# Reordering the eight mLSTM projections, and the squares of the second row tile, in a Trainium2 transformer kernel

## Chip, core and metric

The kernel runs on one core of one Trainium2 chip. The metric is the device time of one execution in microseconds (us), lower is better. The five engines of the core are named as the profile names them: PE (TensorE; PEld is its loading of weights), DVE (VectorE), ACT (ScalarE), POOL (GpSimd) and SP (SyncE, which here only issues DMAs).

## What is computed

Two transformer blocks one behind the other, over 512 positions of 1024 features in float32. The change lies in the first part of the first block, the hybrid mixer:

```
h = rms_norm(x, norm_mix_g)
dq, dk, dv, mq, mk, mv, mo, mi, mf = split(h @ w_in)
y_da = diff_attention(dq, dk, dv)                      # 4 heads
qk   = silu(causal_depthwise_conv([mq, mk]))           # 4 taps, 1024 channels
y_ml = mlstm_chunkwise(qk[:512], qk[512:], mv, mo, mi, mf)   # 4 heads
x    = x + concat(y_da, y_ml) @ w_out
```

In the mLSTM each head multiplies queries with keys, weights the products by gates, multiplies with the values, normalizes, and scales the result by `sigmoid(mo)`. After the mixer come cross-attention over 256 memory rows, a mixture of 32 experts, a norm, and the second block.

## The kernel before

Every float32 product is made of float16 halves: an operand is split into a high half (ACT, line 138) and the remainder (DVE, line 139), and each product is three matmuls (`mm3`, line 110). A weight piece of 1024 x 256 is loaded by SP into a `raw` buffer (line 144) and split in two parts of 128 x 1024 (`load_w`, `wh` and `wl`).

The work stands in program order in `mixer` (line 348): the norm of four row tiles of 128 positions, the projections of the differential attention's values (`values`, line 406) and of its queries and keys (`turned`, line 391), the four heads of the differential attention (`diff_head`, line 520), and `mlstm` (line 583). Then `mem_kv` (line 719) makes keys and values of the memory rows, and `out_proj` (line 477) the output projection.

The order on each engine is not this program order. The framework's scheduler places instructions one after another; of those that its own model takes to be ready, it takes the one that comes first in the program, save where `high_priority` or `after` (line 92: not before these instructions) say otherwise. So while a head of the differential attention waits for DVE or ACT, PE is given matmuls of what comes later in the program: the mLSTM's projections. Each engine is given one list, in the order that comes out of this.

`mlstm` first makes the gates (64 columns), then three kinds of projections, two or four weight pieces each:

- Queries and keys (line 621, four pieces, two blocks of 128 channels each, 24 matmuls of 512 columns a block). A block is followed on ACT by a copy `u` (line 628), a first tap (630), a tanh (635) and a high half, and on DVE by three taps `acc` (line 632), one product `th` (636) and one remainder `mql` (139).
- Values (line 644, two pieces, four row tiles each, 24 matmuls of 256 columns a tile). A tile is followed by one high half on ACT and one remainder `mvl` on DVE.
- Output gates (line 650, two pieces, four row tiles each, 24 matmuls of 256 columns a tile). A tile is followed by one tanh on ACT (`tho`, line 654) and nothing on DVE.

Head h of the mLSTM needs query block h and key block 4 + h, all values, and at its end the output gates. It goes from scores (PE, `tr`), to `W` (DVE, line 678), its halves `ch` and `cl`, and products with the values (PE, `at<-mvh`), to `hr` (DVE, line 699). The PE transposes `tr<-ident,pe` (line 560) and `tr<-ident,yd` (line 474) belong to the differential heads and wait for the DVE rows `pe` (line 553) and `yd` (line 580).

The norm of a row tile (`norm_steps`, line 216) takes two squares with their sums on ACT (line 200), a power on POOL, two scaled halves `xn` on DVE (line 223), eight transposes on PE (line 255), and their halves `xh` (ACT) and `xl` (DVE). Line 357 says which earlier halves a tile's steps wait for.

Of the kernel before, what the change touches and what calls it, by code (L numbers as in the profile page):

```python
# [11 lines left out]
F32 = mybir.dt.float32  # L12
# [8 lines left out]
P = 128  # L21
D = 1024
S = 512
NT = S // P
# [16 lines left out]
W0 = 0, 1  # L41
X0 = 1
LO = 3
EARLY = 0,1,1,1,1,1
WARM = 18
TICKS = [(k, i) for k in range(2) for i in range(NT)], range(14), ((0, 0), (0, 1), (0, 2), (0, 3))
LATE = 2
# [12 lines left out]
def brow(ap):  # L60

    return bass.AP(tensor=ap.tensor, offset=ap.offset, ap=[[0, P], [1, ap.shape[-1]]])


class Kern:
# [192 lines left out]
    def consts(self, low):  # L258
# [23 lines left out]
        pd = self.bank("at")  # L282
        for _ in range(WARM):
            nc.tensor.matmul(pd.rearrange("p (k t) -> p k t", k=4), self.identh,
# [63 lines left out]
    def mixer(self, low, big, pool, early, adp):  # L348
        nc, a = self.nc, self.a
        g = self.g_mix  # L350
        xh = big.tile([P, DC, S], F16, name="xh", tag="A", bufs=2)
        xl = big.tile([P, DC, S], F16, name="xl", tag="A", bufs=2)
        los = []
        ws = []
        with self.tc.high_priority():
            for i in range(NT):
                with self.after(*(self.last_w if i == W0[0] + 2 else ()), *(los[i - 2] if i > 1 else ())):
                    steps = self.norm_steps(low, self.x[i], g, xh, xl, i)
                    next(steps)
                    if i == 0:  # L360

                        ws.append(self.load_w(None, 1024, raw=self.first_w[:, :1024]))
                    for _ in steps:
                        pass
                los.append(self.last)
                if i == W0[0] + 1:
                    with self.after(*los[W0[0]]):
                        ws[0] += self.load_w(None, 1024, raw=self.first_w[:, 1024:])
                if i == W0[1] + 1:
                    with self.after(*los[W0[1]]):  # L370
                        ws.append(self.load_w(a["w_pre"][5]))
        lo = los[LO]
        with self.after(*lo):
            self.mixer_consts(pool)
            self.late_consts()
        ropec = pool.tile([P, S], F32, name="ropec")
        ropes = pool.tile([P, S], F32, name="ropes")
        gateb = pool.tile([64, 1], F32, name="gateb")
        with self.after(*lo):
            nc.scalar.dma_start(ropec, a["rope_cos"])  # L380
            nc.scalar.dma_start(ropes, a["rope_sin"])
            nc.scalar.dma_start(gateb, a["gate_b"])

        mqk = [big.tile([P, 8, S], F16, name=n, tag="C", bufs=2) for n in ("mqh", "mql")]

        qkh = big.tile([P, 8, S], F16, name="qkh", tag="B", bufs=2)
        qkl = big.tile([P, 8, S], F16, name="qkl", tag="B", bufs=2)
        vh = low.tile([P, NT, 512], F16, name="vh", tag="V", bufs=2)
        vl = low.tile([P, NT, 512], F16, name="vl", tag="V", bufs=2)

        def turned(k):
            w = self.load_w(a["w_pre"][k])
            for b in range(2):
                pq = self.proj_feat(w, (xh, xl), 256, b)
                qf = self.t2(pool, "qf", "q")
                nc.scalar.activation(qf, pq, AF.Copy, scale=INV)
                p2 = self.bank("at")
                self.mm(p2, self.swap, qf, True, True)
                t1 = self.t2(pool, "t1", "q")
                nc.gpsimd.tensor_tensor(t1, qf, ropec, OP.mult)  # L400
                t2 = self.t2(pool, "t2", "q")
                nc.vector.tensor_tensor(t2, p2, ropes, OP.mult)
                nc.vector.tensor_tensor(t2, t2, t1, OP.add)
                self.split(t2, qkh[:, 2 * k + b], qkl[:, 2 * k + b], SA)

        def values(k):
            w = ws[k]
            for i in range(NT):
                pv = self.proj_tok(w, (xh, xl), i)
                o = slice(k * 256, k * 256 + 256)  # L410
                self.last = self.split(pv[:, :256], vh[:, i, o], vl[:, i, o], SA * INV)

        self.bank_of_ada = early, "raw"
        self.ada_prio = ADA0
        self.beside = self.ada(adp)

        def ticks():
            for _ in range(next(early_ticks, 0)):
                self.tick()

        early_ticks = iter(EARLY)
        for k in range(2):
            values(k)
            if k == 0:
                self.silu_c(pool)
            ticks()
        for k in range(2):
            turned(k)
            ticks()
            turned(2 + k)  # L430
            ticks()
        lamb = self.t2(pool, "lamb", "q")[:, :256].rearrange("p (a b) -> p a b", a=4)
        nc.scalar.dma_start(lamb.rearrange("p a b -> p (a b)"), brow(a["da_lambda"]))
        lam = self.lam_of(pool, lamb)
        yy = [early.tile([P, DC, S], F16, name=n, tag="raw") for n in ("yyh", "yyl")]
        for h in range(4):
            self.diff_head(low, pool, qkh, qkl, vh, vl, lam, yy, h)
        self.mlstm(pool, xh, xl, *mqk, gateb, yy)
        return yy
# [143 lines left out]
    def mlstm(self, pool, xh, xl, qh, ql, gateb, yy):  # L583
# [33 lines left out]
        nc.scalar.activation(cols[:, 1].rearrange("p k h -> p (k h)"), pc[:, 16:32], AF.Exp)  # L617
        nc.vector.tensor_scalar(cols[:, 1], cols[:, 1], SA, None, op0=OP.mult)


        for k in range(4):
            w = self.load_w(a["w_pre"][6 + k])
            for bb in range(2):
                blk = 2 * k + bb
                pq = self.proj_feat(w, (xh, xl), 256, bb)
                u = pool.tile([P, 3 + S], F32, name="u", tag="u", bufs=2)
                nc.vector.memset(u[:, 0:3], 0.0)
                nc.scalar.activation(u[:, 3:], pq, AF.Copy, scale=INV)
                acc = self.t2(pool, "acc", "q")
                nc.scalar.activation(acc, u[:, 3:], AF.Identity, scale=convw[:, blk, 3:4], bias=convb[:, blk:blk + 1])  # L630
                for j in range(3):
                    nc.vector.scalar_tensor_tensor(acc, u[:, j:j + S], convw[:, blk, j:j + 1], acc,
                                                   op0=OP.mult, op1=OP.add)
                th = self.t2(pool, "th", "q")
                nc.scalar.activation(th, acc, AF.Tanh, scale=0.5)
                nc.vector.scalar_tensor_tensor(th, th, 1.0, acc, op0=OP.add, op1=OP.mult)
                s = 0.5 * SA * (1.0 if blk < 4 else P ** -0.5)
                self.split(th, qh[:, blk], ql[:, blk], s)
# [2 lines left out]
        vl = pool.tile([P, NT, 4, 129], F16, name="mvl")  # L641
        nc.vector.memset(vh[:, :, :, 128:129], 1.0)
        nc.vector.memset(vl[:, :, :, 128:129], 0.0)
        for k in range(2):
            w = self.load_w(a["w_pre"][10 + k])
            for i in range(NT):
                pv = self.proj_tok(w, (xh, xl), i)[:, :256].rearrange("p (h e) -> p h e", h=2)
                self.split(pv, vh[:, i, 2 * k:2 * k + 2, :P], vl[:, i, 2 * k:2 * k + 2, :P], SA * INV)
        tho = pool.tile([P, NT, 512], F32, name="tho")
        for k in range(2):  # L650
            w = self.load_w(a["w_pre"][12 + k])
            for i in range(NT):
                pv = self.proj_tok(w, (xh, xl), i)
                nc.scalar.activation(tho[:, i, k * 256:k * 256 + 256], pv[:, :256], AF.Tanh, scale=0.5 * INV)

        offs = [0, 512, 896, 1152]
        pending = None
        for h in range(4):
# [27 lines left out]
            for g in range(2):  # L686
                pn = self.bank("at")
                pnv = pn[:, :258].rearrange("p (i e) -> p i e", i=2)
                for ii in range(2):
                    i = 2 * g + ii  # L690
# [1298 lines left out]
```

## Time and profile before

| what | value |
|---|---|
| three runs | 1574.32, 1573.76, 1569.97 us |
| median of the runs | 1573.76 us |
| the profiled execution | 1572.59 us |
| its span in the trace | 1570.9 us |
| PE, DVE, ACT busy | 94%, 61%, 38% of the span |
| granted clock of PE, mean | 0.987 |

The profiled execution is 1.17 us below the median. Its span covers the instructions; 1.69 us of its time lie around it. Shares of busy time are means over very different stages, and a stage has to be read by its own window. A busy PE includes time at half clock, which the column PEclk shows (1.00 is 2.4 GHz, 0.50 would be 1.2 GHz).

### The profile page before, as it was taken

How to read it: one execution, taken by the hardware profiler on the slowest of the kernel's cores; microseconds unless marked ns; L12 is line 12 of the kernel's file. 1: busy time of each engine (PE TensorE's matmuls, PEld its weight loads, DVE VectorE, ACT ScalarE, POOL GpSimd, SP SyncE). 2: the span in 40 equal slices, each digit the busy share in tenths (PEclk: the TensorE clock that was granted, in tenths of full speed). 3: DMA queues.
4: the chain of work that ended last, by engine and by line, in shares of the span. 5: the costliest groups of instructions: out<-in, count | busy, mean ns of one | idle time of the engine just before them, and what ended most of it. 6: DMA issues, size and time to landing. Idle time of an engine off the chain costs nothing.

```text
span 1570.9 us, 25373 instructions
## 1 busy us (share of the span) xinstructions
PE 1472.3 (94%) x10268; PEld 815.0 (52%) x10268; DVE 960.3 (61%) x2025; ACT 603.6 (38%) x1256; POOL 102.1 (6%) x120
## 2 busy tenths in 40 slices
PE   8999998899898999999999997898899989989998
PEld 6434676785585444444444443533445774335457
DVE  5769847788855324324324327799475667976562
ACT  5357745423542101101101105642377545226661
POOL 0210001000000000000000002301000012100000
PEclk9999999999999999999999999999999999999999
DMA  8422121788463999999999993232201222340201
GB/s 283 166 81 81 55 81 68 248 339 337 145 265 149 421 421 421 421 421 420 421 421 421 421 420 136 88 111 82 83 28 55 95 75 81 111 128 14 78 28 55
DMA packets 53705, 320.96 MB, mean 204 GB/s; under 512 B 6672, under 2 KB 9552, under 8 KB 17744
## 3 DMA queue, kind: packets, MB, share of 16 engines
q1 hardware_dynamic: 47728, 309.92, 51.0%
q10 hardware_dynamic: 5856, 9.37, 2.1%
q8 instruction: 82, 1.34, 0.3%
q14 instruction: 39, 0.32, 0.1%
HBM read 308.27 MB, written 3.69 MB: 199 GB/s over the span
## 4 chain that ended last, share of the span: by engine, by line
PE 48%; DVE 11%; ACT 4%; issue 3%; DMA 1%; POOL 1%; DVEq 0%; POOLq 0%; ACTq 0%; SPq 0%
PE h L100 13%; PE mm L100 8%; PE y L100 7%; PE cv L100 6%; PE tr L100 3%; PE ga L100 3%; PE at L100 3%; PE po L100 3%; DVE sc L1659 2%; DVE wl L139 2%; DVE m L1658 1%; PE tr L1700 1%; DMA raw<-in_w_big 1%; PE tr L104 1%; DVE sc L1654 1%
## 5 line engine op out<-in xcount | busy, mean ns | idle before, releaser
L100 PE MATMUL h<-raw,xg 128*64 128x512 f32 x1024 | 222.5, 592 | 0.9 <-DVE xg L970 0.9
L100 PEld LDWEIGHTS <-wh 128*128 128x128 f16 x1104 | 107.2, 100 | 134.7 <-issue 41.4
L139 DVE SCALAR_TENSOR_TENSOR wl<-raw,wh 128x1024 f16<-128x1024 f32 (+1 forms) x107 | 134.4, 1263 | 55.5 <-ACT wh L138 55.3
L100 PEld LDWEIGHTS h<-raw,xg 128*64 128x64 f32 x1024 | 73.4, 137 | 146.7 <-issue 141.6
L138 ACT ACTIVATE wh<-raw 128x1024 f16<-128x1024 f32 (+1 forms) x107 | 109.8, 1040 | 75.2 <-PE cv L100 29.7
L1001 DVE SCALAR_TENSOR_TENSOR hm<-hm,h 128x512 f32<-128x512 f32 x16 | 11.0, 687 | 180.5 <-ACT hm L1000 180.5
L100 PE MATMUL y<-raw,hT 128*64 128x512 f32 x512 | 113.6, 595 | 0.0
L1030 DVE SCALAR_TENSOR_TENSOR x<-tr,x 128x512 f32<-128x512 f32 x128 | 86.3, 688 | 11.9 <-PE tr L100 9.9
L100 PEld LDWEIGHTS <-wl 128*128 128x128 f16 x552 | 55.1, 100 | 60.2 <-issue 9.4
L1000 ACT ACTIVATE hm<-h 128x512 f32<-128x512 f32 x16 | 9.6, 597 | 198.5 <-PE h L100 182.8
L100 PE MATMUL cv<-hh,wh 128*128 128x512 f16 x192 | 75.3, 392 | 9.9 <-DVE ga L1388 9.7
L100 PEld LDWEIGHTS <-hh 128*128 128x128 f16 x768 | 72.7, 98 | 15.3 <-ACT hh L138 2.2
L139 DVE SCALAR_TENSOR_TENSOR yl<-y,cw,yh 128x512 f16<-128x512 f32 x32 | 24.0, 751 | 89.0 <-ACT yh L138 89.0
L100 PE MATMUL cv<-hl,wh 128*128 128x512 f16 x192 | 74.9, 390 | 0.0
L100 PE MATMUL cv<-hh,wl 128*128 128x512 f16 x192 | 74.9, 390 | 0.0
L100 PEld LDWEIGHTS y<-raw,hT 128*64 128x64 f32 x512 | 35.2, 137 | 70.3 <-issue 63.8
L100 PEld LDWEIGHTS <-hl 128*128 128x128 f16 x640 | 62.7, 98 | 14.6 <-issue 2.1
L138 ACT ACTIVATE yh<-y,cw 128x512 f16<-128x512 f32 x32 | 22.0, 687 | 114.2 <-PE y L100 112.9
L100 PE MATMUL ga<-Sel,hl 128*128 128x128 f16 x480 | 65.8, 219 | 0.0
L100 PE MATMUL ga<-Sel,hh 128*128 128x128 f16 x480 | 65.7, 219 | 0.0
L1295 DVE CUSTOM_DVE_ANT_0 raw<-raw,cact 128x1024 f32<-128x1024 f32 x48 | 58.7, 1240 | 8.0 <-DMA raw<-in_w_ada 7.1
L100 PE MATMUL mm<-wh,xh 128*128 128x256 f16 x192 | 53.7, 280 | 2.5 <-ACT xh L138 2.4
(437 smaller groups left out, 3422.6 us busy)
## 6 DMA issues: line engine op xcount, KB each, us to landing
raw<-in_w_moe SPq DMA_DIRECT2D x192, 1024.0 KB, 19.8
raw<-in_w_pre SPq DMA_DIRECT2D x33, 1024.0 KB, 4.9
raw<-in_w_big SPq DMA_DIRECT2D x30, 1024.0 KB, 5.0
raw<-in_w_ada SPq DMA_DIRECT2D x24, 1024.0 KB, 7.0
R<-cu ACTq DMA_DIRECT2D x16, 271.0 KB, 6.6
R<-cu SPq DMA_DIRECT2D x16, 271.0 KB, 7.0
x<-in_x_tm SPq DMA_DIRECT2D x4, 512.0 KB
t5d<-t5v SPq DMA_DIRECT2D x1, 1536.0 KB, 10.9
```

The lines of the kernel that those rows point to most:

```text
L100: self.last_mm = self.pin(self.nc.tensor.matmul(out, lhsT, rhs, start=start, stop=stop, skip_group_check=True))
L104: return self.pin(self.nc.tensor.transpose(out, src, ident))
L138: return (nc.scalar.activation(hi, src, func, scale=scale), nc.vector.scalar_tensor_tensor(lo, src, scale, hi, op0=OP.mult, op1=OP.subtract))
L139: nc.vector.scalar_tensor_tensor(lo, src, scale, hi, op0=OP.mult, op1=OP.subtract))
L1000: nc.scalar.activation(hm[:n], ph[0][:n], AF.Tanh, scale=0.5 / SA)
L1001: nc.vector.scalar_tensor_tensor(hm[:n], hm[:n], 1.0, ph[0][:n], op0=OP.add, op1=OP.mult)
L1030: self.last_add = nc.vector.scalar_tensor_tensor(xo, pc, 1.0 / 1024.0, xo, op0=OP.mult, op1=OP.add)
L1295: nc.vector.tensor_tensor_reduce(w, w, cact, 1.0, 0.0, OP.mult, OP.add, to)
L1654: nc.vector.scalar_tensor_tensor(sc, re[:, :W], s, sc, op0=OP.mult, op1=OP.add)
L1658: nc.vector.max(m8, sc)
L1659: nc.vector.match_replace(sc, m8, sc, -3.0e38)
L1700: nc.tensor.transpose(pt[:, (i - k) * P:(i - k + 1) * P], ps_[i][:, k * P:(k + 1) * P], self.ident)
```

## The change

A table `MLSTM` sets the order of the eight projections by kind (0 values, 1 queries and keys, 2 output gates) and piece: both values; the first piece of queries (heads 0, 1) and of keys (heads 0, 1); both output gates; the second piece of queries (heads 2, 3) and of keys. Before it was four of queries and keys, two of values, two of output gates. The computation is the same. In line 357 the second row tile's steps (i = 1) now wait for the first tile's last halves; before, only tiles 2 and 3 had such a wait, for the tile two before.

```diff
+MLSTM = (0, 0), (0, 1), (1, 0), (1, 2), (2, 0), (2, 1), (1, 1), (1, 3)
...
             for i in range(NT):
-                with self.after(*(self.last_w if i == W0[0] + 2 else ()), *(los[i - 2] if i > 1 else ())):
+                with self.after(*(self.last_w if i == W0[0] + 2 else ()), *(los[max(i - 2, 0)] if i else ())):
                     steps = self.norm_steps(low, self.x[i], g, xh, xl, i)
...
-        for k in range(4):
+        def queries_keys(k):
+
             w = self.load_w(a["w_pre"][6 + k])
             for bb in range(2):
                 blk = 2 * k + bb
...
-        for k in range(2):
+        tho = pool.tile([P, NT, 512], F32, name="tho")
+
+        def values(k):
             w = self.load_w(a["w_pre"][10 + k])
...
-        tho = pool.tile([P, NT, 512], F32, name="tho")
-        for k in range(2):
+
+        def output_gates(k):
             w = self.load_w(a["w_pre"][12 + k])
...
+        for step, k in MLSTM:
+            (values, queries_keys, output_gates)[step](k)
```

What it does to the order on PE, counted there: projection matmuls of 256 and of 512 columns between the last `yd` transposes of one differential head and those of the next, and (in brackets) those of them that stand directly ahead of the `yd` transposes, behind the head's last product with values.

| stretch | before: 256 | before: 512 | after: 256 | after: 512 |
|---|---|---|---|---|
| head 0 | 0 | 70 (24) | 124 (28) | 0 |
| head 1 | 0 | 91 (20) | 68 (0) | 29 (10) |
| head 2 | 81 (28) | 31 | 29 (29) | 67 (5) |
| head 3 | 144 (22) | 0 | 149 (32) | 0 |
| behind head 3, ahead of the mLSTM's heads | 159 | 0 | 14 | 96 |

The first place is ACT at the start of the program (`x_82` to `x_85` are the four row tiles, `junk,ss` the squares). Before:

```order
L200 ACTIVATE junk,ss<-x_82 128x512 x2
L138 ACTIVATE wh<-raw 128x1024
L200 ACTIVATE junk,ss<-x_83 128x512 x2
L138 ACTIVATE xh<-tr 128x4x128 x2
L138 ACTIVATE wh<-raw 128x1024
L200 ACTIVATE junk,ss<-x_84 128x512 x2
```

and after:

```order
L201 ACTIVATE junk,ss<-x_82 128x512 x2
L139 ACTIVATE wh<-raw 128x1024
L139 ACTIVATE xh<-tr 128x4x128 x2
L201 ACTIVATE junk,ss<-x_83 128x512
L139 ACTIVATE wh<-raw 128x1024
L201 ACTIVATE junk,ss<-x_83 128x512
L201 ACTIVATE junk,ss<-x_84 128x512 x2
```

The second tile's squares have gone behind the first tile's halves, and its second square also behind the split of the next weight part.

The second place is DVE around the end of differential head 0 and the start of head 1. Before:

```order
L578 TENSOR_SCALAR rs_r<-rs_r 128x4
L632 SCALAR_TENSOR_TENSOR acc<-u,mlc,acc 128x512
L580 TENSOR_TENSOR yd<-at,rs_r 128x512
L550 RECIPROCAL sm<-sm 128x2
L632 SCALAR_TENSOR_TENSOR acc<-u,mlc,acc 128x512
L551 TENSOR_SCALAR sm<-sm,lam 128x1
L632 SCALAR_TENSOR_TENSOR acc<-u,mlc,acc 128x512
L139 SCALAR_TENSOR_TENSOR yyl<-tr,gs,yyh 128x512
L553 SCALAR_TENSOR_TENSOR pe<-pe,sm 128x128
```

and after:

```order
L579 TENSOR_SCALAR rs_r<-rs_r 128x4
L581 TENSOR_TENSOR yd<-at,rs_r 128x512
L551 RECIPROCAL sm<-sm 128x2
L140 SCALAR_TENSOR_TENSOR mvl<-mm,mvh 128x2x128
L552 TENSOR_SCALAR sm<-sm,lam 128x1
L554 SCALAR_TENSOR_TENSOR pe<-pe,sm 128x128
```

Three taps of a convolution block that stood between the head's rows are gone from here, and one values' remainder has come.

The third place is DVE at the start of the mLSTM's head 0 (`ml` and `xn` belong to the norm of the memory rows). Before:

```order
L678 TENSOR_TENSOR W<-tr,W 128x512
L678 TENSOR_TENSOR W<-tr,W 128x384
L678 TENSOR_TENSOR W<-tr,W 128x256
L139 SCALAR_TENSOR_TENSOR cl<-W,ch 128x512
L139 SCALAR_TENSOR_TENSOR cl<-W,ch 128x384
L139 SCALAR_TENSOR_TENSOR ml<-mm,mh 128x4x128
L139 SCALAR_TENSOR_TENSOR cl<-W,ch 128x256
```

and after:

```order
L685 TENSOR_TENSOR W<-tr,W 128x512
L633 SCALAR_TENSOR_TENSOR acc<-u,mlc,acc 128x512
L140 SCALAR_TENSOR_TENSOR ml<-mm,mh 128x4x128 x2
L140 SCALAR_TENSOR_TENSOR cl<-W,ch 128x512
L633 SCALAR_TENSOR_TENSOR acc<-u,mlc,acc 128x512
L685 TENSOR_TENSOR W<-tr,W 128x384
L685 TENSOR_TENSOR W<-tr,W 128x256
L637 SCALAR_TENSOR_TENSOR th<-th,acc 128x512
L140 SCALAR_TENSOR_TENSOR cl<-W,ch 128x384
L140 SCALAR_TENSOR_TENSOR cl<-W,ch 128x256
L140 SCALAR_TENSOR_TENSOR mql<-th,mqh 128x512
```

The last convolution block's rows now stand among the rows of the mLSTM's first head. On PE, eight transposes of the memory rows now stand ahead of this head's first product with the values; before there were five.

## Rows read from the trace of the kernel before

**Rows 1.** The page's first part: busy time and share of the span by engine.

```profile
PE 1472.3 (94%) x10268; PEld 815.0 (52%) x10268; DVE 960.3 (61%) x2025; ACT 603.6 (38%) x1256; POOL 102.1 (6%) x120
```

**Rows 2.** Busy time by stage: differential heads 0 to 3, output gates, mLSTM's heads.

```profile
core 0: us, PE busy (x) PEld busy (x) DVE busy (x) ACT busy (x) POOL busy (x), PEclk, DMA share, GB/s
...
93.00:126.00 33.00, 29.77 (x176) 13.85 (x173) 25.05 (x60) 22.43 (x48) 1.88 (x2) 0.95 0.15 55
126.00:155.00 29.00, 27.64 (x171) 13.41 (x167) 27.28 (x59) 22.83 (x47) 1.92 (x1) 1.00 0.29 96
155.00:180.00 25.00, 23.47 (x188) 14.95 (x185) 23.10 (x54) 17.77 (x41) 1.43 (x1) 1.00 0.17 59
180.00:206.00 26.00, 23.69 (x217) 18.64 (x216) 19.34 (x44) 17.56 (x41) 2.13 (x3) 1.00 0.23 81
206.00:226.40 20.40, 20.40 (x172) 17.66 (x171) 3.37 (x5) 5.82 (x11) 0.00 (x0) 0.92 0.15 53
226.40:291.00 64.60, 57.61 (x469) 41.75 (x468) 51.74 (x109) 35.77 (x84) 8.20 (x8) 0.95 0.31 105
```

**Rows 3.** What PE waited for from 93 to 207 us, the two longest: total, times, longest.

```profile
PE tr L560 <- DVE pe L553: 4.7, 5, 1.9
PE tr L474 <- DVE yd L580: 2.3, 2, 1.3
```

**Rows 4.** The same from 207 to 345 us, the three longest in total.

```profile
PE mm L100 <- DVE kk L139: 1.9, 1, 1.9
PE mm L255 <- DVE ml L139: 1.9, 1, 1.9
PE tr L100 <- DVE W L678: 1.7, 3, 0.8
```

**Rows 5.** Busy time in three short stretches with a low PEclk.

```profile
100.00:105.80 5.80, 5.58 (x21) 2.25 (x21) 3.65 (x10) 5.63 (x14) 0.00 (x0) 0.71 0.00 0
...
207.00:214.00 7.00, 7.00 (x50) 5.66 (x50) 0.92 (x3) 0.95 (x3) 0.00 (x0) 0.76 0.01 2
...
238.00:246.00 8.00, 6.62 (x40) 5.32 (x41) 7.28 (x14) 4.56 (x12) 1.10 (x2) 0.57 0.56 199
```

**Rows 6.** DVE by line and form, 93 to 207 us: busy, mean ns | idle before.

```profile
L632 DVE SCALAR_TENSOR_TENSOR acc<-u,mlc,acc 128x512 f32<-128x512 f32 x24 | 17.8, 743 | 0.0
L139 DVE SCALAR_TENSOR_TENSOR wl<-raw,wh 128x1024 f16<-128x1024 f32 x13 | 15.8, 1219 | 0.9 <-ACT wh L138 0.9
L636 DVE SCALAR_TENSOR_TENSOR th<-th,acc 128x512 f32<-128x512 f32 x8 | 5.5, 688 | 0.8 <-ACT th L635 0.6
L139 DVE SCALAR_TENSOR_TENSOR mql<-th,mqh 128x512 f16<-128x512 f32 x8 | 5.5, 685 | 0.0
...
L139 DVE SCALAR_TENSOR_TENSOR mvl<-mm,mvh 128x256 f16<-128x256 f32 x8 | 3.4, 423 | 0.2
```

**Rows 7.** ACT's timeline around 217 us: start, duration.

```profile
216.11 0.38 ACT L654 ACTIVATE tho<-mm 128x256 f32<-128x256 f32 x1 [0.25 <-PE mm L100]
...
218.73 0.38 ACT L654 ACTIVATE tho<-mm 128x256 f32<-128x256 f32 x1 [1.29 <-PE mm L100]
```

**Rows 8.** The chain that ended last, near 1070 us: start, duration.

```profile
1070.25 5.18 PE mm L100 x24
```

**Rows 9.** Timeline at the start: ACT, PE and DVE.

```profile
10.83 0.63 ACT L200 ACTIVATE junk<-x 128x512 bf16<-128x512 f32 x1 [0.55 <-DMA x<-in_x_tm]
...
12.21 1.06 ACT L138 ACTIVATE xh<-tr 128x512 f16<-128x512 f32 x2
...
14.03 1.40 DVE L223 SCALAR_TENSOR_TENSOR xn<-x,rs_r,grow 128x512 f32<-128x512 f32 x2
```

**Rows 10.** DVE's timeline in the mLSTM's head 0.

```profile
229.55 1.16 DVE L678 TENSOR_TENSOR W<-tr,W 128x512 f32<-128x512 f32 x2 [0.37 <-PE tr L100]
...
234.63 0.42 DVE L699 SCALAR_TENSOR_TENSOR hr<-at,dn 128x256 f32<-128x256 f32 x1
```

**Rows 11.** The costliest groups of the whole span, the first row.

```profile
L100 PE MATMUL h<-raw,xg 128*64 128x512 f32 x1024 | 222.5, 592 | 0.9 <-DVE xg L970 0.9
```

## The prediction

> **What bounds the kernel now.** I began with the page's busy shares: PE is busy for 94% of the span, DVE for 61% [rows 1]. So PE is the bound nearly everywhere, and an order of the same work can only win time in which PE idles or runs at half clock. Next I read the windows of the stages the change touches [rows 2]. In the four differential heads PE is idle for 33.00 - 29.77 = 3.23, 1.36, 1.53 and 2.31 us, together 8.43 us. In the stretch of the output gates behind them it never idles, although DVE works there for only 3.37 of 20.40 us. In the mLSTM's heads it idles for 64.60 - 57.61 = 6.99 us. The third view, PE's waits, says for what: from 93 to 207 us 4.7 us are waits for DVE's `pe` and 2.3 for its `yd`, the ends of a head's chains [rows 3]; behind that the longest are for DVE's `kk`, `ml` and `W` [rows 4]. No DMA stands in these rows. Last come the stretches with a low granted clock [rows 5]: 0.71 over 5.8 us, 0.76 over 7.0 and 0.57 over 8.0 lose 0.29 x 5.8 = 1.7, 1.7 and 3.4 us, since part of each ran at 1.2 GHz instead of 2.4.
>
> A gain or loss here reaches the end in full. The experts' stage later holds the chain, and there the main matmuls waited 0.9 us in 1024 instructions [rows 11]: PE starts that stage earlier or later by what is won or lost now.
>
> The reader should see one thing more in rows 2. DVE is busy for 76% of head 0, 94% of head 1, 92% of head 2 and 74% of head 3. PE idles least in the two heads where DVE is fullest. The waits come from the length of a head's own chain (reduce, exponential, reciprocal, scale, transpose), not from DVE being full.
>
> **The projections' order.** Each instruction of the projections stays: PE's matmuls, ACT's and DVE's splits, the eight weight loads, and no load of ACT's tables is added. A block of queries or keys costs DVE 3 x 0.743 + 0.688 + 0.685 = 3.6 us, a tile of values 0.42, a tile of output gates nothing [rows 6]. On PE 24 matmuls of 256 columns take 218.73 - 216.11 = 2.62 us [rows 7], 0.109 each, and 24 of 512 take 5.18 us [rows 8], 0.216 each.
>
> Head 0 keeps its order until its last tile, so its waits of 3.23 us stay. Ahead of its `yd` transposes 24 matmuls of 512 columns (5.2 us) become 28 of 256 (3.1 us): less cover for the same chain, but DVE's taps have left it too. I put that at nothing.
>
> Head 1 loses the convolution. Its filling falls from 91 x 0.216 = 19.7 us to 68 x 0.109 + 29 x 0.216 = 13.7 us. The head gets shorter, but PE's work per head chain gets thinner, as it was in head 3 (144 x 0.109 = 15.7 us of filling, DVE at 74%), which idled for 2.31 us. I take head 3's value for it: 1.36 becomes 2.31.
>
> Head 2 takes most of the convolution (67 of 512 columns) and becomes what heads 1 and 2 were: 1.45, the mean of their idle times, for 1.53. Head 3 is filled by 149 matmuls of output gates, which put no work on DVE, with 32 instead of 22 ahead of its `yd` transposes, 10 x 0.109 = 1.1 us more cover; I take 2.31 - 0.9 = 1.4.
>
> The sum of the heads is 3.23 + 2.31 + 1.45 + 1.4 = 8.4, so **0.0**. Its ends: all idle time of heads 1 to 3 gone, -5.2 us; or every head at head 0's 3.23, +4.5 us.
>
> Behind head 3, 159 matmuls of output gates (17.3 us) become 14 of those and 96 of 512 columns (1.5 + 20.7 = 22.2 us), the rest having gone into the heads. Four blocks and four weight parts give DVE work below PE's here, and ACT likewise, so **0.0**; that PE's idle DVE is now used wins nothing, because PE never waited there [rows 2].
>
> In the mLSTM's head 0 the last block's two taps, `th` and `mql` now stand on DVE between the first `W` and the first `hr`: 2 x 0.743 + 0.688 + 0.685 = 2.9 us. Before, this path took from 229.55 to 234.63, 5.1 us [rows 10]. PE waits behind each of those rows with its products with the values; the three transposes of the memory rows brought forward cover a few tenths. In return the `ml` rows stand earlier, for which PE waited 1.9 us [rows 4]. Of 2.9 us I take 2.4 as new waits and 1.5 of the 1.9 as gone: **+0.9**, ends 0 and +4.3 (the 2.9 and one `xn` and one `ml` that also moved ahead, 0.7 each as an `xn` in rows 9, with nothing gained).
>
> **The second tile's squares.** Before, ACT squared tile 1 from 10.83 us and wrote tile 0's halves only from 12.21 [rows 9]; the squares are those 1.4 us. Now the halves go first and the first projection can start up to 1.4 us earlier. But DVE still splits the first weight part ahead of the remainders, and tile 1's `xn`, at 14.03 before, waits for its second square, now behind the split of another weight part on ACT and that part's remainder on DVE, 1.2 us [rows 6]. Counting the split like the remainder, tile 1 comes up to 2.4 us later. I take **0.0**, between the ends -1.4 and +2.4, as both lie on the same few rows of PE.
>
> **Queues.** On SP the loads keep their order up to the memory rows; behind, some loads for the second block's modulation change places with projection weights. POOL's powers move by one place. PE waits for neither there [rows 3, 4], so 0.
>
> **The clock.** The stretch of 0.71 begins behind the longest wait for `pe` (1.9 us), that of 0.76 behind a wait for `yd` (1.3), that of 0.57 behind the wait for `ml` (1.9) [rows 3 to 5]. I keep waits of that size in all three places, so **0.0**, with 3.4 us to either side. The Trainium skill (TensorE: Matmul & The Clock Gate, "Loop structure matters more than you think") marks VectorE's copies out of PSUM as not breaking the array's warmth. This trace does not agree: the low clocks of rows 5 follow waits for DVE. By that rule the clock's 1.7 us would fall out of both rivals below, which would then give 1568.3 and 1576.9 us.
>
> Sum: +0.9. Against the profiled execution's 1572.59 us that is **1573.5 us**, 0.3 below the median of the runs (1573.76), which lies 1.17 us above that execution. About 0.3%, 4.7 us, can be told from no change.
>
> **Rivals.** *DVE's relief does shorten the waits.* Heads 1 and 3 no longer share DVE with taps; if the tap rows ahead of `pe` and `yd` made those waits, the 5.2 us go, and one low stretch of 1.7 with them: 1573.5 - 6.9 = 1566.6. For it: every wait in rows 3 is for DVE, and the rows of the second place in the change stand shorter now. Against: head 3, with little on DVE, idled more than heads 1 and 2.
>
> *The convolution's tail blocks the mLSTM's first head* (the other side). DVE's order puts the last block among that head's rows; where cover on PE runs out, each us of them is a us of PE. It decides if the first `cl` comes more than about 1 us after PE has done the scores and the transposes it was given. All 4.3 us and another low stretch of 1.7 against my 0.9: 1573.5 + 5.1 = 1578.6. For it: DVE is busy for 51.74 of 64.60 us there already [rows 2]. Against: three memory transposes more stand ahead of the first product with the values, as cover. The Trainium skill (PSUM — Partial Sum Buffer, "Engine vs sequencer instructions") calls VectorE's queue strictly first in, first out. By that rule nothing of the blocked rows can slip past the taps, which is this rival in full; no row here shows a case to test it.
>
> *The start gets slower*: tile 1 comes 2.4 us later and nothing is won before it, 1573.5 + 2.4 = 1575.9, still no change.
>
> **Numbers.** Forecast 0.50; slower start 0.12; relief 0.25, since the waits are on the right engine and the low clock can add to it; blocked head 0.13. So faster 0.25, same 0.62, slower 0.13. The range takes in the relief's time nearly and the block's wholly, and the ends of the start and the clock: 1567.0 to 1579.5.
>
> **What would show it.** Right: PE idle of about 8 us over the four differential heads; no idle behind head 3 with DVE busy there; a wait of about 2 us for `cl` or `W` in the mLSTM's first head; first projection before 12 us but tile 1's `xn` after 15. Wrong: idle time in the heads under 5 us or no low clock from 93 to 250 us (relief), or over 10 us of idle in the mLSTM's heads (block).

## The result and the profile after

The changed kernel took 1581.47 us (median of 16 runs, 1573.55 to 1586.73) where the kernel before took 1573.91 beside it: a ratio of 1.0055, 95% interval 1.004 to 1.007. A second comparison gave 1.0047 (1.0029 to 1.0066). So the change makes the kernel slower by about 8 us, a little more than the 4.7 us that can be told from no change. The forecast was 1573.5 us, and its range ended at 1579.5.

The profiled execution took 1583.46 us with a span of 1581.8. First the page's busy shares, which answer to [rows 1]:

```profile
span 1581.8 us, 25378 instructions
...
PE 1481.0 (94%) x10268; PEld 815.9 (52%) x10268; DVE 961.3 (61%) x2025; ACT 603.2 (38%) x1256; POOL 101.6 (6%) x120
```

The same instructions, the same busy times on DVE and ACT, and PE 8.7 us busier than in [rows 1]. No matmul was added, so PE's rows got longer, which goes with the granted clock of the two executions, 0.982 against 0.987 in the mean. The stages, as in [rows 2], now read so (the start; differential heads 0 to 3; the projections behind them; the mLSTM's heads up to the last `hr` transposes; from there to the first product with `wo`):

```profile
core 0: us, PE busy (x) PEld busy (x) DVE busy (x) ACT busy (x) POOL busy (x), PEclk, DMA share, GB/s
0.00:17.50 17.50, 12.36 (x56) 6.07 (x57) 7.29 (x18) 9.12 (x19) 2.51 (x11) 1.00 0.85 301
...
93.80:126.40 32.60, 27.91 (x223) 18.89 (x220) 23.13 (x56) 20.19 (x46) 1.40 (x2) 0.95 0.21 72
126.40:149.40 23.00, 21.81 (x173) 13.89 (x173) 14.88 (x40) 13.57 (x33) 1.01 (x1) 1.00 0.19 67
149.40:176.90 27.50, 25.96 (x173) 13.93 (x174) 24.44 (x54) 20.06 (x43) 1.91 (x1) 1.00 0.16 52
176.90:203.20 26.30, 23.90 (x214) 18.34 (x214) 18.41 (x43) 16.55 (x41) 2.09 (x3) 1.00 0.19 68
203.20:231.30 28.10, 28.05 (x130) 14.48 (x130) 15.28 (x23) 13.00 (x19) 0.00 (x0) 0.88 0.22 76
231.30:295.70 64.40, 56.96 (x469) 40.78 (x468) 53.48 (x116) 39.57 (x90) 9.03 (x8) 0.97 0.30 107
295.70:316.80 21.10, 18.02 (x148) 15.41 (x149) 14.87 (x23) 8.04 (x10) 0.61 (x4) 0.92 0.80 299
```

PE idles for 32.60 - 27.91 = 4.69 us in head 0, then 1.19, 1.54 and 2.40: 9.82 us, against 8.43 before (in the second traces of both kernels, taken below as e5 and e6, 10.9 against 9.0). Behind the heads it is never idle. In the mLSTM's heads it idles 7.44 us, before 6.99. These differences are small. Against them stand the starts of PE's landmarks: the mLSTM's head 0 begins 4.9 us later than before (231.35 against 226.48), the first product with `wo` 8.1 us later (316.82 against 308.75), the experts' first `h` 8.2 us later (501.23 against 492.99); in the second traces 4.2, 7.6 and 5.6 us. PE's waits, which answer to [rows 3] and [rows 4] (engine, line, what it waited for: us in total, times, longest):

```profile
PE tr L475 <- DVE yd L581: 4.2, 3, 1.8
PE tr L561 <- DVE pe L554: 3.9, 4, 1.8
PE tr L475 <- DVE sm L551: 1.2, 1, 1.2
...
PE tr L101 <- DVE W L685: 3.4, 6, 0.8
PE tr L475 <- DVE hr L720: 3.1, 1, 3.1
PE mm L101 <- DVE vv L140: 3.0, 1, 3.0
PE at L101 <- ACT ch L139: 0.5, 1, 0.5
```

Two things are new above the "...": the waits for `yd` grew from 2.3 to 4.2 us and are three instead of two. Below it the 1.9 for `ml` and the 1.9 for `kk` of [rows 4] are gone, and in their place stand one wait of 3.1 us for `hr` and, in this execution, 3.0 us for `vv` (1.3 before).

**How runs are compared below.** Each execution has a mean granted clock, and time follows it: before's 104 runs with a known clock lie between 1565.0 and 1580.3 us, at 0.982 to 0.991. A fit over all some 240 runs of this study, with one level for each kernel and one slope for all, gives 1.0 us for each 0.001 of mean clock (0.7 to 1.2 for each kernel by itself) and leaves 1.5 us of scatter. The changed kernel lies 5.5 us (interval 0.7 to either side) above before *at equal clock*; and its 28 runs had a mean clock of 0.983 against before's 0.986, which is the other 3 us. The price is an average over the kernel and its executions, so this split is the fit's. The experiments are read by both.

### The profile page after: what moved, and what is told of

Read it like the earlier page. It is cut to its first block, busy times and chain, and to the rows that moved or that the text cites. A ratio compares the mean times of both kernels' runs of the same rounds, so it can differ in the third digit from the quotient of the medians.

```text
span 1581.8 us, 25378 instructions
## 1 busy us (share of the span) xinstructions
PE 1481.0 (94%) x10268; PEld 815.9 (52%) x10268; DVE 961.3 (61%) x2025; ACT 603.2 (38%) x1256; POOL 101.6 (6%) x120
## 4 chain that ended last, share of the span: by engine, by line
PE 47%; DVE 11%; ACT 3%; issue 3%; DMA 2%; POOL 1%; SPq 0%; DVEq 0%; ACTq 0%; POOLq 0%
PE h L101 13%; PE mm L101 8%; PE y L101 7%; PE cv L101 5%; PE tr L101 3%; PE ga L101 3%; PE at L101 3%; PE po L101 2%; DVE wl L140 2%; DVE sc L1666 2%; DVE m L1665 2%; PE tr L1707 1%; DMA raw<-in_w_big 1%; PE tr L105 1%; DVE sc L1661 1%
```

## The experiments

Each table row is one kernel, named by the first part of its label; "equal clock" is its level in that fit against before, with the half width of its 95% interval. In the orders, V0 and V1 are the two pieces of the values, Q0 and Q1 of the queries, K0 and K1 of the keys, G0 and G1 of the output gates; in the code these are (0, 0) and (0, 1), (1, 0) and (1, 1), (1, 2) and (1, 3), (2, 0) and (2, 1). Q1 and K1 are the "second" or "late" pieces.

| label | order | start | runs | ratio to before (95%) | mean clock | equal clock, us |
|---|---|---|---|---|---|---|
| before | Q0 Q1 K0 K1 V0 V1 G0 G1 | old | 104 | 1 | 0.986 | 0 |
| change | V0 V1 Q0 K0 G0 G1 Q1 K1 | new | 16 | 1.0055 (1.004 to 1.007) | 0.983 | +5.6 ± 0.8 |
| e5 | the same | new | 12 | 1.0047 (1.0029 to 1.0066) | 0.983 | +5.3 ± 1.0 |
| e1 | the same | old | 6 | 1.0055 (1.0034 to 1.0077) | 0.984 | +6.0 ± 1.3 |
| e2 | as before | new | 12 | 0.9998 (0.9982 to 1.0014) | 0.987 | +0.3 ± 0.9 |
| e3 | V0 V1 Q0 Q1 K0 K1 G0 G1 | old | 12 | 1.0027 (1.0011 to 1.0042) | 0.985 | +2.9 ± 0.9 |
| e4 | Q0 K0 V0 V1 G0 G1 Q1 K1 | old | 12 | 1.0000 (0.9982 to 1.0019) | 0.987 | +1.0 ± 0.9 |
| e7 | Q0 V0 V1 K0 G0 G1 Q1 K1 | old | 12 | 1.0012 (0.9992 to 1.0032) | 0.985 | +1.8 ± 0.9 |
| e8 | Q0 V0 V1 Q1 K0 K1 G0 G1 | old | 12 | 1.0004 (0.9986 to 1.0021) | 0.985 | -0.5 ± 0.9 |
| e12 | Q0 V0 V1 K0 G0 Q1 K1 G1 | old | 12 | 0.9993 (0.9978 to 1.0008) | 0.988 | +0.6 ± 0.9 |
| e9 | as e8 | new | 12 | 0.9981 (0.9964 to 0.9998) | 0.989 | 0.0 ± 0.9 |
| e14 | as e8 | new | 12 | 1.0024 (1.0004 to 1.0043) | 0.985 | +0.7 ± 0.9 |
| e13 | as e12 | new | 12 | 1.0009 (0.9994 to 1.0025) | 0.986 | +0.3 ± 0.9 |

e9 and e14 are the same kernel, and their ratios differ by 0.43% with intervals that do not meet. So one comparison of 12 runs can miss by 0.2%; at equal clock the two agree within 0.7 us. That the change is slower rests on three comparisons (change, e5 and, for its order alone, e1), all above 1.0045.

### Which part of the change: the order, the start, and two halves of the order

The first four kernels take the change apart. e1 keeps the order and takes back the start, e2 the reverse:

```diff
 e1, against the changed kernel
-  with self.after(..., *(los[max(i - 2, 0)] if i else ())):
+  with self.after(..., *(los[i - 2] if i > 1 else ())):
 e2, against the changed kernel
-MLSTM = (0, 0), (0, 1), (1, 0), (1, 2), (2, 0), (2, 1), (1, 1), (1, 3)
+MLSTM = (1, 0), (1, 1), (1, 2), (1, 3), (0, 0), (0, 1), (2, 0), (2, 1)
```

e3 (values first, nothing else late) and e4 (second pieces late, values not first) each do one half of the order, with the old start:

```diff
 e3
+MLSTM = (0, 0), (0, 1), (1, 0), (1, 1), (1, 2), (1, 3), (2, 0), (2, 1)
 e4
+MLSTM = (1, 0), (1, 2), (0, 0), (0, 1), (2, 0), (2, 1), (1, 1), (1, 3)
```

> The changed order of the projections with the old start (tile 1's squares ahead of tile 0's halves). Theory 'late blocks' (the second query and key pieces end up behind head 3, their convolution rows stand on VectorE among mLSTM head 0's rows): 6 to 8 us slower than before, and the trace shows the same +4 us from head 3's yd to mLSTM head 0 and +3 us more up to the first wo product. Theory 'light heads' (values first leave heads 0 and 1 with chains that show): 2 to 3 us slower, lying between 94 and 150 us. Theory 'front' (the squares edit costs by itself and shifts the rest): clearly faster than the changed kernel, by 1 us or more. Theory 'clock' (only the granted clock is lower): at the same mean granted clock as before the same time within 1.5 us.

> The old order with the new start (second tile's squares behind the first tile's halves). Theories 'late blocks' and 'light heads': 0 to 1 us slower than before. Theory 'front': 0.7 us slower at 94 us, 1 to 3 us at the end. First projection near 10.3 us instead of 12.9, PE then waits more for weight halves and tile 1, and mask_q comes 0.3 to 0.9 us later than before.

> Values first, then the four query and key pieces in their old sequence, then the output gates; old start. Heads 0 and 1 get nearly the same filling as in the changed kernel, but nothing of the convolution is left behind head 3. Theory 'late blocks': within 1.5 us of before, tail and mLSTM head 0 as before. Theory 'light heads': 1.5 to 3 us slower than before, and PE waits more from 94 to 150 us. Theory 'clock': time goes with the granted clock alone.

> First query and key pieces in their old place, values and output gates in the middle, the second query and key pieces last; old start. The convolution's last 96 matmuls of 512 columns stand behind head 3 as in the changed kernel, but the first heads are filled with convolution. Theory 'late blocks': 4 to 5 us slower than before, with waits for W, hr or vv of mLSTM head 0 and on. Theory 'light heads': within 1 us of before, or faster. Theory 'clock': time goes with the granted clock alone, the tail with a stretch at 1.2 GHz of about 7 us.

Measured: e1 1579.26 us (1577.91 to 1586.31), ratio 1.0055; e2 0.9998; e3 1.0027; e4 1.0000. The theory that I held most, "late blocks", expected 4 to 5 us for e4 and nothing for e3, and it got it the wrong way round: "light heads" named the half that costs more of the two, and its 1.5 to 3 us for e3 were measured (2.9 at equal clock). But e1's 6.0 at equal clock is what "late blocks" expected of it, and twice what "light heads" did: neither half is the whole, and 2.9 and 1.0 do not add up to 6.0. "Clock" falls too, as e1 and e3 are slower at equal clock. "Front" falls: the start alone gives 0.3 ± 0.9, and the order with the old start loses as much as the whole change.

Why did the late pieces not block the mLSTM's head 0? On DVE they stand there as predicted. But behind them the scheduler gave PE other work: between the first `nM` and the first `hr` transposes PE does 47 matmuls of the memory rows' keys (`mm<-mh,wh` and its two companions) where it did 28 before, and from the third to the fourth head's `hr` transposes it needs 13.6 us instead of 17.9. Cover was pulled forward, and head 3 of the mLSTM lost it.

### Head 0's cover

All traces with the values first (change, e5, e1, e3) show a wait of 1.4 us for `yd` in head 0; the ten other traces (two of them of the kernel before) show none there. Around it, on ACT and DVE of the changed kernel (start, duration, engine, line, operation; in brackets the idle time ahead and its releaser):

```profile
122.09 0.59 ACT L575 ACTIVATE sq<-at 128x512 f32<-128x512 f32 x1
122.23 1.23 DVE L140 SCALAR_TENSOR_TENSOR wl<-raw,wh 128x1024 f16<-128x1024 f32 x1 [0.51 <-ACT wh L139]
123.37 0.68 DVE L577 TENSOR_REDUCE s<-sq 128x4 f32<-128x512 f32 x1
124.08 0.17 DVE L171 TENSOR_SCALAR rs_t<-s 128x4 f32<-128x4 f32 x1
125.38 0.17 DVE L579 TENSOR_SCALAR rs_r<-rs_r 128x4 f32<-128x4 f32 x1 [1.13 <-POOL rs_r L172]
125.66 0.69 DVE L581 TENSOR_TENSOR yd<-at,rs_r 128x512 f32<-128x512 f32 x1
```

The same chain in the kernel before:

```profile
120.13 0.58 ACT L574 ACTIVATE sq<-at 128x512 f32<-128x512 f32 x1
121.22 0.68 DVE L576 TENSOR_REDUCE s<-sq 128x4 f32<-128x512 f32 x1
124.35 0.69 DVE L580 TENSOR_TENSOR yd<-at,rs_r 128x512 f32<-128x512 f32 x1
```

The taps are gone from this chain, but a weight part's remainder (1.23 us) stands ahead of `s` instead. From the start of `sq` to the end of `yd` it takes 126.35 - 122.09 = 4.26 us, where it took 125.04 - 120.13 = 4.91: 0.65 us shorter. From `s` on it is 2.98 us (before 3.82), 1.13 of them a wait for POOL's power. As cover PE has 28 matmuls of 256 columns, 3.1 us, where it had 24 of 512, 5.2 us. So 2.1 us of cover went for 0.65 us of chain, and the difference is the 1.4 us of wait. e7 and e8 put the first query piece ahead of the values, which gives head 0 44 matmuls of 256 and 2 of 512 columns as cover, 5.2 us again; e5 and e6 repeat the changed kernel and the kernel before unaltered, for a second trace each.

```diff
 e7, against e1
+MLSTM = (1, 0), (0, 0), (0, 1), (1, 2), (2, 0), (2, 1), (1, 1), (1, 3)
 e8, against e3
+MLSTM = (1, 0), (0, 0), (0, 1), (1, 1), (1, 2), (1, 3), (2, 0), (2, 1)
```

> The changed kernel unaltered, for a second trace and more times. Theory 'stalls': its loss of about 5.6 us at equal granted clock is made of waits that stand in every execution, so PE again waits about 1.6 us for yd in head 0, 2.0 us for yd in head 3 and 3.2 us for hr in the last mLSTM head; the 3.2 us for vv at 306 us, which the order-only kernel had at 0.8, was a late weight load of one execution and comes back at 0.8. Theory 'queue' (the moved loads delay the output weights each time): the vv wait is 3 us again. Times: median 1579 to 1583 us, mean granted clock lower than before's by about 0.002 to 0.003.

> The kernel before unaltered, for a second trace. No wait for yd in head 0, 1.5 us in head 3, 2.0 us for ml and 2.1 us for kk in the mLSTM heads, each within 0.3 us of the first trace; the stretches at 1.2 GHz fall partly elsewhere (in its first trace 101.9, 207.7 and 238.4 us). If the stretches are where they were, the clock is a property of the order; if not, the longest waits only make them likelier.

> The changed order with the first query piece put ahead of the values, old start: head 0 then has 44 matmuls of 256 and 2 of 512 columns ahead of its yd (5.2 us of cover, as before the change) where the changed order had 28 of 256 (3.1 us). Late pieces as in the changed order. Theory 'head 0's cover': the yd wait of head 0 goes (1.6 us to under 0.3), and the kernel is within 2 us of before at equal granted clock, against 6.0 for the order alone. Theory 'late blocks': still 4 to 6 us slower. Theory 'values anywhere': head 1, now filled with values, waits 1.5 us or more for its yd, and the loss stays 3 us or more.

> The first query piece, then the values, then the other three pieces in sequence, then the output gates; old start. Head 0's cover is as in the run beside it, nothing of the convolution stands behind head 3. Theory 'head 0's cover': 0 to 1 us slower than before at equal granted clock (values first without this piece: 2.9). Theory 'values anywhere': 2 to 3 us slower. Theory 'late blocks': 1.5 us or more below the run beside it, which differs only in where the second pieces stand.

Measured: e7 1.0012, e8 1.0004, e5 1.0047; e6 gave one time, 1573.09 us. Its trace repeats the waits of the first within 0.3 us, but for the two for `pe` in head 0 (1.9 and 1.3 us in the first, 1.5 and 2.3 here). Of the three stretches of [rows 5] with time at 1.2 GHz those near 207 and 240 us are there again, the one near 102 is not. Moving that one piece gives back 6.0 - 1.8 = 4.2 us at equal clock in one order and 2.9 + 0.5 = 3.4 in the other. The same four runs read the other way price the late pieces: 6.0 - 2.9 = 3.1 us from e3 to e1 and 1.8 + 0.5 = 2.3 from e8 to e7, more than e4's 1.0. So "late blocks" had its 1.5 us or more between e8 and e7, but not its 4 to 6 us for e7. PE's waits in head 0, e3 above and e8 below:

```profile
PE tr L561 <- DVE pe L554: 3.0, 2, 1.5
PE tr L475 <- DVE yd L581: 1.4, 1, 1.4
PE mm L101 <- DVE mvl L140: 0.7, 2, 0.3
PE at L101 <- ACT pe L548: 0.3, 1, 0.3
```

```profile
PE tr L561 <- DVE pe L554: 2.9, 2, 1.6
```

The 1.4 for `yd` is gone with 0.7 for `mvl` (tiles of values that PE's banks wait for) and 0.3 for ACT: 2.4 us, most of the pair's 3.4. For e1 and e7 the same view over all four heads gives 10.4 and 9.4 us, which is 1.0 of 4.2 (the differences 3.4 and 4.2 carry 1.2 and 1.5 us of uncertainty). All of PE's idle time, from the start of head 0 to the first product with `wo`, of e1, e7, e3 and e8:

```profile
93.60:312.93 219.33, 199.83 (x1528) 134.31 (x1524) 164.37 (x349) 130.99 (x280) 16.09 (x19) 0.98 0.28 99
96.30:314.49 218.19, 200.58 (x1525) 134.80 (x1524) 164.29 (x350) 131.18 (x280) 15.54 (x19) 0.97 0.29 100
94.10:311.61 217.51, 199.18 (x1526) 134.10 (x1525) 164.46 (x350) 130.20 (x280) 15.20 (x19) 0.98 0.28 97
92.90:308.52 215.62, 199.44 (x1527) 134.62 (x1524) 164.32 (x350) 131.37 (x280) 16.08 (x19) 0.97 0.28 97
```

PE idles 19.50, 17.61, 18.33 and 16.18 us there: the cover is worth 1.9 and 2.1 us of idle time, the late pieces 1.2 and 1.4, about half of what the times say. "Values anywhere" falls with e8: its head 1 is filled with values alone, waits 1.1 us for its `yd`, and the kernel is no slower than before.

The second trace of the changed kernel repeats the waits: 4.5 us for `yd`, 3.1 for `hr`, 3.5 for `W`. Only `vv` is back at 0.6, as it was in e1: the 3.0 belonged to one execution, in which a late load held the output weights' halves on ACT and DVE, and `vv` stood behind them on DVE. The queue theory falls.

### One long wait instead of two

In the mLSTM's last head the late pieces turn two waits, for `kk` and for `hr`, into one. e12 is e7 with one piece of the gates moved to the end; then no convolution row stands in the mLSTM's heads, and on PE these read as in the kernel before.

```diff
 e12, against e7
+MLSTM = (1, 0), (0, 0), (0, 1), (1, 2), (2, 0), (1, 1), (1, 3), (2, 1)
```

> As the run with the first query piece ahead of the values and the second pieces late (+1.7 us at equal clock, +2.8 as measured), but with one piece of the output gates moved to the very end: no convolution row stands in the mLSTM's heads any more, whose instructions then stand as in the kernel before. Theory 'one long wait' (the late pieces do not add idle time, they join the wait for kk of 2 us and that for hr of 1.2 us in the last mLSTM head into one of 3.3 us, behind which the clock falls): kk and hr waits are apart again, no stretch at 1.2 GHz between 285 and 305 us, mean granted clock 0.001 higher, and 1 to 3 us faster than that run. Theory 'late pieces' by themselves: no faster than that run. Rival: head 3 filled with 12 matmuls of 512 columns ahead of yd waits longer than the 1.5 us of that run, and gives the gain back.

Measured: e12 0.9993, 4 us less than e7 in the mean of the runs (1571.2 against 1575.4), but at equal clock only 1.2 ± 1.3; the rest goes with the granted clock, 0.9877 against 0.9847, and two sets of runs of one kernel (e9 and e14) differ by more than that. The rival, a longer wait in head 3, did not come (1.1 us). PE's waits in the mLSTM's heads, e7 above and e12 below:

```profile
PE tr L101 <- DVE W L685: 3.2, 6, 0.8
PE tr L475 <- DVE hr L720: 3.1, 1, 3.1
PE mm L101 <- DVE vv L140: 0.6, 1, 0.6
PE at L101 <- ACT ch L139: 0.5, 1, 0.5
```

```profile
PE mm L101 <- DVE kk L140: 2.4, 1, 2.4
PE mm L256 <- DVE ml L140: 1.9, 1, 1.9
PE mm L101 <- DVE vv L140: 1.7, 1, 1.7
PE tr L101 <- DVE W L685: 1.6, 3, 0.7
```

The totals do not differ in favour of e12. What differs is the longest piece, and the stretch behind it. The window from the last `hr` transposes to the first `wo` product (span, PE busy with its instructions, PEld, DVE, ACT, POOL, granted clock, DMA, GB/s), of e7, e5 and e8:

```profile
295.80:314.50 18.70, 18.05 (x149) 15.44 (x150) 14.58 (x23) 8.10 (x10) 0.62 (x4) 0.91 0.82 308
```

```profile
299.00:317.40 18.40, 17.72 (x148) 15.42 (x149) 14.56 (x22) 8.09 (x10) 0.61 (x4) 0.92 0.82 310
```

```profile
289.50:308.50 19.00, 17.35 (x156) 15.30 (x157) 14.59 (x23) 9.65 (x12) 0.66 (x4) 1.00 0.76 274
```

Part of the stretch ran at 1.2 GHz in e7 and e5, none in e8. This holds over the study: right behind the one wait of 3.1 us the clock fell in four of five traces (e1, e4, e5, e7; in the changed kernel's first trace it fell a little later, behind the 3.0 for `vv`). Where `kk` and `hr` are waited for apart (1.5 to 1.9 and 1.0 us), it fell in none of eight. In e12's own trace the wait for `kk` grew to 2.4 us, and behind that it fell too, so the expectation of no such stretch there was missed. So in this place the one long wait goes with a stretch at 1.2 GHz, which costs 0.08 x 18.4 = 1.5 us. Elsewhere the length of the wait does not tell: behind the 1.9 us for `ml` the clock fell in four of nine traces, and in the five with late pieces, which have no wait above 0.8 us there, it fell in all five. Behind a wait of 2.3 us for `pe` in head 0 it fell in three of eight, behind head 3's wait for `yd` of 1.1 to 2.1 us in twelve of fourteen.

### Is there a version that beats both?

e9 joins e8's order with the new start, e13 e12's order with it (each is the changed kernel with the one line of that order), and e14 repeats e9.

> The first query piece, then values, the other pieces in sequence, output gates (the order that stood 0.6 us below before at equal granted clock) together with the new start. If the two edits add up (new start alone: +0.2): within 1 us of before at equal clock, ratio 0.998 to 1.001, so no version beats the kernel before by what can be told. If the new start shifts the heads unfavourably, as theory 'front' has it: 1 to 3 us slower. Waits: the sum of head 0's waits for pe under 5 us and no yd wait there.

> The order with one piece of the output gates at the end (ratio 0.9993 to before) together with the new start. If the new start really gives something with these orders, as the run of the second-place values with it hinted (ratio 0.9981 against 1.0004 without), the ratio is 0.997 to 0.998. If that hint was the granted clock of its executions, the ratio is 0.998 to 1.001 and at equal clock within 1 us of before.

> The same kernel as the run of the second-place values with the new start (ratio 0.9981, interval 0.9964 to 0.9998, mean granted clock 0.9885). If it is faster by itself, the ratio stays at 0.998 or below and the clock high; if those executions only happened to get more clock, the ratio is 0.999 to 1.0005.

Measured: e9 1570.00 us, 0.9981; e13 1573.47, 1.0009; e14 1575.33, 1.0024, above what either reading expected of it. e9's gain was its clock (0.9885, in the repeat 0.9848). All orders without the two faults (thin cover in head 0, late pieces) lie within 1 us of before at equal clock, and none beats it.

## Why the prediction was wrong

**Head 0: the step that failed first.** The prediction set 3.1 us of cover for 5.2 "at nothing", because the taps had left the chain. But a weight part's remainder took the taps' place ahead of `s`, and the chain got only 0.65 us shorter for 2.1 us less cover. Head 0's idle went from 3.23 to 4.69 us (in the second traces from 4.06 to 5.42), and the piece that restores the cover is worth 3.4 and 4.2 us at equal clock. The term's upper end took head 0's 3.23 us as the worst that any head could come to; that head 0 itself could grow was left out.

**Head 3.** Predicted were 1.4 us of idle for 2.31, with ten matmuls more as cover; measured 2.40. The cover is there. But the norm of the memory rows moved into this head's chain; under "Queues" the prediction had counted only POOL's powers as moved, at nothing. On DVE of the changed kernel:

```profile
199.02 0.75 DVE L224 SCALAR_TENSOR_TENSOR xn<-raw,rs_r,grow 128x512 f32<-128x512 f32 x1 [0.67 <-POOL rs_r L184]
199.69 0.68 DVE L577 TENSOR_REDUCE s<-sq 128x4 f32<-128x512 f32 x1
200.29 0.74 DVE L224 SCALAR_TENSOR_TENSOR xn<-raw,rs_r,grow 128x512 f32<-128x512 f32 x1
200.94 0.16 DVE L171 TENSOR_SCALAR rs_t<-s 128x4 f32<-128x4 f32 x1
...
202.23 0.17 DVE L579 TENSOR_SCALAR rs_r<-rs_r 128x4 f32<-128x4 f32 x1 [1.06 <-POOL rs_r L172]
202.50 0.69 DVE L581 TENSOR_TENSOR yd<-at,rs_r 128x512 f32<-128x512 f32 x1
```

One `xn` (0.75) stands ahead of `s` and one (0.74) between `s` and `rs_t`; from the start of `sq` (198.07) to the end of `yd` it takes 5.1 us, before 3.6. In e7, where they come later, the wait for `yd` in head 3 is 1.3 us, here 1.8 behind 1.1 us more of cover. Heads 1 and 2 came out at 1.19 and 1.54 us, for a forecast of 2.31 and 1.45. So the heads' term is +1.4 of idle instead of 0.0.

**The tail.** Right as far as it went: no idle (28.05 of 28.10 us) with DVE busy for 15.28. What a longer stretch can lose to the clock was not looked at: it runs at 0.88 over 28.1 us where before it was 0.92 over 20.40 [rows 2], 3.4 us lost instead of 1.6. A second trace of the kernel before also has 7 us at 1.2 GHz there, so this difference is not shown to belong to the change.

**The mLSTM's first head.** +0.9 was forecast, as 2.4 us of new waits less 1.5 of the one for `ml`. Measured: the wait for `ml` is gone wholly, and 0.8 for `W`, 0.5 for `ch` and two more for `W` (0.2 and 0.7) replace it, in sum 2.2 us; the term is +0.3. The rival "blocked head" is refuted as a mechanism (idle 7.44 us in the mLSTM's heads, under its 10): its time of 1578.6 came nearest, but by luck. The late pieces do cost something, 1.0 to 3.1 us at equal clock, only not as that block. The Trainium skill (PSUM — Partial Sum Buffer, "Engine vs sequencer instructions") calls VectorE's queue strictly first in, first out. The rows agree as far as they show it: in the changed kernel the first `W` stands right behind a late tap, for which DVE itself sat idle 0.62 us, and PE waits 0.8 us for that `W`.

```profile
235.07 0.75 DVE L633 SCALAR_TENSOR_TENSOR acc<-u,mlc,acc 128x512 f32<-128x512 f32 x1 [0.62 <-ACT acc L631]
235.74 0.68 DVE L685 TENSOR_TENSOR W<-tr,W 128x512 f32<-128x512 f32 x1
...
244.28 0.42 DVE L706 SCALAR_TENSOR_TENSOR hr<-at,dn 128x256 f32<-128x256 f32 x1
```

DVE's path from the first `W` to the first `hr` grew from 5.1 [rows 10] to 8.5 us, 3.4 more where 2.9 was forecast. What made the block cheap is PE's own list, which got other work ahead of it.

**The start.** 0.0 with both ends was right: first projection at 10.33 us (before 12.85), tile 1's `xn` at 15.62 instead of 14.03, alone worth 0.3 ± 0.9.

**The clock: the second step that failed.** It was set at 0.0 for "I keep waits of that size in all three places", with 3.4 us to either side. The change put one wait of 3.1 us in place of 1.9 and 1.0, and one of 1.4 in head 0 that was not there, and the mean clock went from 0.986 to 0.983, some 3 us. That these waits made all of that is not shown. By the clock records of the traces the changed kernel has 17 and 20 us at 1.2 GHz between head 0 and the first `wo` product, where the kernel before has 14 and 10; behind the experts' first `h`, where all matmuls stand in the same order in both kernels, it has 34 and 41 against 24 and 24. The cause of that larger part stays open. The Trainium skill (TensorE: Matmul & The Clock Gate, "Loop structure matters more than you think") marks VectorE's copy out of PSUM as not breaking the array's warmth, in a loop whose next matmuls follow immediately. The prediction held its trace against that; but here PE stood still for DVE's rows, up to 3.1 us for `hr`, which is not that case, so no run here shows the rule.

**What the sum comes to.** At equal clock 5.5 us: 3.4 to 4.2 for head 0's cover, 1.0 to 3.1 for the late pieces (e4: 1.0 ± 0.9; e7 against e12: 1.2 ± 1.3; e7 against e8: 2.3 ± 1.2; e1 against e3: 3.1 ± 1.5), nothing for the start. Then 3 us of clock. What stays open: only about half of the 5.5 us stands as idle time of PE in the traces (20.4 and 19.0 us from head 0 to the first `wo` product, before 16.7 and 17.2), and the runs do not split the 3 us of clock between head 0's wait, the one for `hr` (e4 has the latter, with a clock no lower than before's) and the stages far behind.

## What to carry to other kernels

When work is reordered that only fills the gaps of another chain, count the filling in microseconds at the place where that chain ends, and look up what the scheduler puts into the slots that come free on the chain's engine: here a weight part's remainder and a norm's `xn` took them, so that one chain got 0.65 us shorter for 2.1 us less cover, and another 1.5 us longer. And read the granted clock place by place and in more than one trace: neither the total of PE's waits nor the longest of them told here where it would fall.

## What the runs showed of the hardware

The price of the clock over a whole kernel was even: some 1.0 us for each 0.001 of mean granted clock, 0.7 to 1.2 in the single kernels. Executions of one kernel differed by up to 0.014 in it (e5: 0.977 to 0.991) and so by 16 us, although in the kernels traced twice nearly all waits repeat within some tenths (not the ones for `vv` and `pe` named above); and even the means of 12 executions of one kernel differed by 0.004 (e9 and e14), 4 us. Differences under half a per cent are told in this kernel only with the clock of each run beside its time.
